# Long convolutions by FFT: complex sums of every second frequency pair left to the inverse transform's matmuls, and the first frequency's correction on ACT and GpSimd

## The chip, the cores and the metric

The kernel runs on one core of a Trainium2 chip. A core has five engines with a queue each, served in order: PE (TensorE, matmuls), DVE (VectorE), ACT (ScalarE), POOL (GpSimd) and SP (SyncE, which issues DMAs). The metric is the device time of one execution in microseconds (us).

## The reference, cut to what matters

The program is one trunk layer of a hybrid backbone: a combined input projection, a Mamba-2 scan and beside it a Hyena branch with two long convolutions, an output projection, and a retrieval over 16384 single-neuron experts. The change touches the long convolutions alone:

```
def long_conv_bidir(u, h_fwd, h_bwd, bias):
    seqlen = u.shape[1]                       # 1024 tokens, 1024 channels
    k = jnp.concatenate([h_fwd, jnp.zeros_like(h_fwd[:1]), h_bwd[:0:-1]], axis=0)
    k_f = jnp.fft.rfft(k, axis=0)
    u_f = jnp.fft.rfft(u.astype(jnp.float32), n=2 * seqlen, axis=1)
    y = jnp.fft.irfft(u_f * k_f, n=2 * seqlen, axis=1)[:, :seqlen]
    return (y + u.astype(jnp.float32) * bias.astype(jnp.float32)).astype(u.dtype)

def hyena(proj_hy, short_w, short_b, filters, filt_bias, norm_g, rows):
    u = dwconv_centred(proj_hy, short_w, short_b)
    v, x1, x2 = jnp.split(u, 3, axis=-1)
    z = x1 * long_conv_bidir(v, filters[0, 0], filters[0, 1], filt_bias[0])
    z = colmajor_to_raster(
        long_conv_bidir(raster_to_colmajor(z, rows), filters[1, 0], filters[1, 1], filt_bias[1]), rows)
    return group_rmsnorm(x2 * z, norm_g, HY_HEADS)
```

The product `u_f * k_f` is complex. Frequency 0 is a special case: its spectrum and that of the highest frequency are both real, and the kernel keeps the two in the real and the imaginary part of one entry.

## The kernel before

**Stages.** The program goes through the input projection (with the convolution filters beside it), then the scan, the convolutions and the first part of the output projection beside each other, and then the rest of the output projection and the experts. The filters' spectra lie in DRAM by the time the convolutions begin.

**A convolution job.** The channels are worked on in 8 blocks of W = 128, for each of two convolutions: 16 jobs. In a job the 1024 tokens stand as a tile of 128 partitions with 8 blocks of 128 channels. A butterfly over the 8 blocks (`butterfly`, DVE with GpSimd for two subtractions over three blocks each and ACT for two scalings) makes 8 pairs of real and imaginary input, one by one; the loop in `convs` sends each pair through three steps:

- `product`, the way forward: four fp32 matmuls of 128x128 with the matrices dft_f make the pair's spectrum hx in PSUM. The trace has two records for each such matmul.
- `spectrum`: one DVE product (L993) multiplies hx with the filter's spectrum h_k and writes h_m, which holds four blocks of 128 columns: for the real and the imaginary part (r) two terms each (j). For pair 0 of a job (n == 0) two DVE instructions on partition 0 alone (L997, L998) put frequency 0 right. Then one DVE add (L1000) sums the two terms of each part into h_p.
- `back`, the way back: four matmuls of 128x128 with dft_i add up into hy in PSUM, two for each half of hy. `take` (ACT and DVE) collects the results of 8 pairs, and `finish` (L954, L955, on GpSimd) multiplies by the gate h_g.

LAGS = (0, 1, 1) holds the second and the third step back by one pair each. h_m had NM = 2 buffers, h_p NP = 3, hx and hy NX = 2 each.

**Beside it.** `mix` runs the jobs beside three other streams: the scan (tiles s_...; its last sum on a group is L649), the search keys (ke, wq) and, once the scan is over, the first parts of the output projection (`out_some`: weights are scaled in L1091, split by ACT and GpSimd into wo_h and wo_l in `split`, L50 and L51; the matmuls are L1131 into pe, and DVE adds pe to the row in L1134, two adds for each block of 128 tokens, 32 in all). The second of these parts reads finished outputs of the convolutions (d_ohy, loaded into ot_o).

**Order.** Rates (CS, KR, TR, TL) set how many pairs the program issues beside a step of the other streams, but the order on each engine is then made by a scheduler that goes through the instructions with estimated times. It is fixed when the kernel is built; on the chip each queue is served in that order.

Of the kernel before, what the change touches and what calls it, by code (L numbers as in the profile page):

```python
# [15 lines left out]
AF = mybir.ActivationFunctionType  # L16
# [656 lines left out]
class Hyena:  # L673
# [296 lines left out]
    def convs(self):  # L970

        K, nc, wk, ps, W = self.K, self.K.nc, self.wk, self.ps, self.W
        n = D // W
        jobs = []
        for q in range(n + LQ):
            if q < n:
                jobs.append((0, q))
            if q >= LQ:
                jobs.append((1, q - LQ))
        todo = [[], [], []]  # L980

        def product(j, n, A):
            fw = self.tiles(self.PAIRS[n])[0]
            x = ps.tile([128, 2, W], F32, name="hx", bufs=NX)
            for r in range(2):
                self.mm(x[:, r], [(fw[2 * r + k], A[:, k]) for k in range(2)], "dft_f")
            return x

        def spectrum(j, n, x):

            kr = j["k"][:, 1, n]
            t = wk.tile([128, 2, 2, W], F32, name="h_m", bufs=NM)
            nc.vector.tensor_tensor(t, x[:, None].to_broadcast([128, 2, 2, W]),  # L993
                                    bass.AP(tensor=kr.tensor, offset=kr.offset,
                                            ap=[kr.ap[0], [-8 * W, 2], [8 * W, 2], [1, W]]), op=ALU.mult)
            if n == 0:
                nc.vector.tensor_scalar_mul(t[:1, 1, 1], t[:1, 0, 1], -1.0)  # L997
                nc.vector.memset(t[:1].rearrange("p r j c -> p (r j) c")[:, 1:3], 0.0)  # L998
            P = wk.tile([128, 2, W], F32, name="h_p", bufs=NP)
            nc.vector.tensor_add(P, t[:, :, 0], t[:, :, 1])  # L1000
            return P

        def back(j, n, t):
            iv = self.tiles(self.PAIRS[n])[1]
            x = ps.tile([128, 2, W], F32, name="hy", bufs=NX)
            for r in range(2):
                self.mm(x[:, r], [(iv[2 * r + k], t[:, k]) for k in range(2)], "dft_i")
            self.take(j, n, x)
            if n == 7:
                self.finish(j)  # L1010

        steps = (product, spectrum, back)
        lags = LAGS

        def advance(item):

            todo[0].append(item)
            for s in range(3):
                if len(todo[s]) > (lags[s] if item is not None else 0):
                    x = todo[s].pop(0)  # L1020
                    if x is None:
                        y = None
                    else:
                        y = steps[s](*x)
                    if s < 2:
                        todo[s + 1].append(None if x is None else (x[0], x[1], y))

        nxt = self.load(*jobs[0])
        for k in range(len(jobs)):
            j = nxt  # L1030
            if k + 1 < len(jobs):
                later = jobs[k + 1]
            for n, A in enumerate(self.butterfly(j["u"])):
                advance((j, n, A))
                if n == NL and k + 1 < len(jobs):
                    nxt = self.load(*later)
                yield
        while any(todo):
            for s in range(3):
                if todo[s]:  # L1040
                    x = todo[s].pop(0)
                    y = steps[s](*x)
                    if s < 2:
                        todo[s + 1].append((x[0], x[1], y))
            yield
# [1 line left out]

LF = 2
NA = 4
NM = 2  # L1050
NP = 3
NX = 2
NK = 2
NL = 5
# [866 lines left out]
```

## Time and profile before

| what | value |
|---|---|
| time, median of 3 runs | 4224.18 us (4220.09 to 4227.6) |
| the profiled execution's own time | 4237.9 us |
| its span, first to last instruction | 4236.2 us |
| PE busy | 3768.2 us, 89% of the span |
| DVE busy | 3415.0 us, 81% |
| POOL busy | 2054.5 us, 48% |
| ACT busy | 1389.0 us, 33% |
| mean granted clock of PE | 0.948 of full speed |

Busy shares are means over stages with different limits, so the windows further down are the better guide to the convolutions' stretch. A granted clock of 1.00 is TensorE's upper level (2.4 GHz), and a mean below that is time spent at the lower one (1.2 GHz). PE's busy time includes modelled ends of matmuls; the spacing of starts back to back is the better price of one.

### The profile page before, as it was taken

The numbers are of one execution on the slowest core, as the hardware profiler recorded it, in microseconds if no ns is written. First come the engines' busy times: TensorE is split into PE (matmuls) and PEld (weight loads), VectorE is DVE, ScalarE is ACT, GpSimd is POOL, SyncE is SP. The second block draws the span as 40 slices with busy tenths as digits, with TensorE's granted clock in tenths as the row PEclk, the third lists the DMA queues.
The fourth block names the chain that finished last, engine by engine and source line by source line (L and its number), as shares of the span: only waits on it lengthen the run. The fifth ranks groups of instructions, "written<-read, shape, count | busy, mean of one in ns | idle before, by whom it ended". The sixth has DMA issues, their size and how long they took to land.

```text
span 4236.2 us, 59519 instructions
## 1 busy us (share of the span) xinstructions
PE 3768.2 (89%) x21481; PEld 3306.9 (78%) x21481; DVE 3415.0 (81%) x6093; ACT 1389.0 (33%) x2658; POOL 2054.5 (48%) x1627
## 2 busy tenths in 40 slices
PE   5999999898887897789999877999989999989995
PEld 4787887777777786689999866888878878878884
DVE  5665887556889795589999996888878888878998
ACT  3233333325553221232236665222222222222221
POOL 2232323244434221056435444666767767767775
PEclk8999999998898998899999998999999999999998
DMA  6333433467774545567536545899989999989997
GB/s 209 103 123 103 130 112 131 136 194 208 237 232 140 165 156 166 181 226 272 209 135 220 201 169 203 316 319 325 345 294 340 326 319 335 348 305 339 344 322 258
DMA packets 509670, 974.06 MB, mean 230 GB/s; under 512 B 33771, under 2 KB 291231, under 8 KB 506432
## 3 DMA queue, kind: packets, MB, share of 16 engines
q1 hardware_dynamic: 395616, 557.25, 40.1%
q0 software_dynamic: 110880, 405.98, 26.1%
q10 hardware_dynamic: 2880, 7.03, 0.5%
q8 instruction: 169, 2.77, 0.3%
q14 instruction: 125, 1.02, 0.1%
HBM read 823.20 MB, written 146.95 MB: 229 GB/s over the span
## 4 chain that ended last, share of the span: by engine, by line
DVE 21%; PE 21%; DMA 12%; issue 7%; POOL 5%; ACT 1%; SPq 0%; POOLq 0%; DVEq 0%; ACTq 0%
PE x_acc L1671 10%; PE x_s L1631 7%; DMA x_vr<-in_peer_v_dram 6%; DVE rows L1532 3%; POOL rows L1508 2%; DMA rows<-in_peer_u_dram,ids 2%; PE pe L1131 2%; DVE r_e L1456 2%; DVE e_p L1545 1%; POOL x_vl L1603 1%; DVE r_e L1454 1%; DVE r_tmp L1343 1%; DVE r_oh L1420 1%; DVE x_ul L1592 1%; DMA rows<-in_peer_v_dram,ids 1%
## 5 line engine op out<-in xcount | busy, mean ns | idle before, releaser
L1631 PE MATMUL x_s<-fTh,x_uh 128*128 128x320 f32 x2048 | 639.6, 312 | 9.0 <-ACT x_a L1632 8.9
L1631 PE MATMUL x_s<-fTh,x_ul 128*128 128x320 f32 x2048 | 638.7, 312 | 5.9 <-DVE x_ul L1592 5.9
L1631 PE MATMUL x_s<-fTl,x_uh 128*128 128x320 f32 x2048 | 639.2, 312 | 0.0
L1671 PE MATMUL x_acc<-x_vl,x_ah 128*128 128x512 f32 x1280 | 515.9, 404 | 14.6 <-POOL x_vl L1603 14.4
L1671 PE MATMUL x_acc<-x_vh,x_ah 128*128 128x512 f32 x1280 | 448.5, 403 | 89.8 <-ACT x_vh L1602 67.0
L1545 DVE SCALAR_TENSOR_TENSOR e_p<-rows,e_a,e_p 128x1024 f32<-128x1024 f32 x381 | 489.6, 1285 | 29.3 <-DMA rows<-in_peer_v_dram,ids 22.2
L1671 PE MATMUL x_acc<-x_vh,x_al 128*128 128x512 f32 x1280 | 511.4, 401 | 0.0
L1508 POOL DMA_INDIRECT rows<-in_peer_u_dram,ids x384 | 416.1, 1084 | 173.0 <-DVE rows L1532 55.7
L1532 DVE SCALAR_TENSOR_TENSOR rows<-rows,e_p 128x1024 f32<-128x1024 f32 x384 | 455.1, 1208 | 38.5 <-DMA rows<-in_peer_u_dram,ids 38.0
L1508 POOL DMA_INDIRECT rows<-in_peer_v_dram,ids x384 | 398.9, 1039 | 146.1 <-DVE e_p L1545 64.6
L1603 POOL TENSOR_TENSOR x_vl<-x_vr,x_vh 128x512 fp32r<-128x512 f32 x256 | 339.5, 1330 | 192.7 <-ACT x_vh L1602 182.7
L1631 PEld LDWEIGHTS x_s<-fTh,x_uh 128*128 128x128 f32 x2048 | 388.3, 190 | 22.0 <-ACT x_a L1632 12.9
L1631 PEld LDWEIGHTS x_s<-fTh,x_ul 128*128 128x128 f32 x2048 | 388.5, 190 | 15.5 <-DVE x_ul L1592 6.7
L1631 PEld LDWEIGHTS x_s<-fTl,x_uh 128*128 128x128 f32 x2048 | 388.7, 190 | 9.6
L1671 PEld LDWEIGHTS x_acc<-x_vh,x_ah 128*128 128x128 f32 x1280 | 242.1, 194 | 141.9 <-ACT x_vh L1602 74.4
L1671 PEld LDWEIGHTS x_acc<-x_vl,x_ah 128*128 128x128 f32 x1280 | 248.5, 194 | 68.7 <-POOL x_vl L1603 22.7
L1602 ACT ACTIVATE x_vh<-x_vr 128x512 fp32r<-128x512 f32 x256 | 159.5, 627 | 431.6 <-DMA x_vr<-in_peer_v_dram 362.3
L1671 PEld LDWEIGHTS x_acc<-x_vh,x_al 128*128 128x128 f32 x1280 | 248.3, 194 | 49.3
L1592 POOL TENSOR_TENSOR x_ul<-x_raw,x_uh 128x1024 fp32r<-128x1024 f32 x57 | 140.9, 2472 | 275.9 <-ACT x_uh L1591 274.6
L199 PE MATMUL mm<-xh,whi 128*128 128x512 f32 (+1 forms) x784 | 265.4, 414 | 6.4 <-DVE acc L235 3.4
L199 PE MATMUL mm<-xl,whi 128*128 128x512 f32 (+1 forms) x784 | 264.6, 412 | 7.1 <-DVE xl L51 7.1
L199 PE MATMUL mm<-xh,wlo 128*128 128x512 f32 (+1 forms) x784 | 264.1, 412 | 0.4 <-POOL wlo L51 0.4
(380 smaller groups left out, 8528.3 us busy)
## 6 DMA issues: line engine op xcount, KB each, us to landing
x_raw<-in_peer_uT_dram SPq DMA_DIRECT2D x128, 512.0 KB
x_vr<-in_peer_v_dram SPq DMA_DIRECT2D x256, 256.0 KB
d_G<-r_st SPq DMA_DIRECT2D x20, 2048.0 KB
x_g<-d_G SPq DMA_DIRECT2D x32, 1280.0 KB
wraw<-in_w_mod_dram SPq DMA_DIRECT2D x32, 1024.0 KB
wraw<-in_w_in_dram SPq DMA_DIRECT2D x24, 1024.0 KB
wk_w<-d_WK SPq DMA_DIRECT2D x24, 1024.0 KB
d_kr<-h_k SPq DMA_DIRECT2D x32, 512.0 KB
```

The source lines that it names most:

```text
L199: nc.tensor.matmul(p, w[:, k], x[j][:, k, t0:t0 + n], start=(k == 0 and q == 0), stop=(k == 7 and q == 2))
L1131: nc.tensor.matmul(p, a[:, k], w[:, ss], start=(k == 0 and q == 0), stop=(k == n - 1 and q == 2))
L1343: V.match_replace(work, vals[:, 0:8], src, -3.0e38)
L1456: V.tensor_tensor(e2, io, T[:, 1, ts, None].to_broadcast([128, 8, 128]), op=ALU.is_equal)
L1508: nc.gpsimd.indirect_dma_start(out=r, out_offset=None, in_=table, in_offset=bass.IndirectOffsetOnAxis(ap=ids[:, j:j + 1], axis=0))
L1532: nc.vector.scalar_tensor_tensor(r, r, 1.0, f, op0=ALU.mult, op1=ALU.mult, accum_out=d[:, j:j + 1])
L1545: nc.vector.scalar_tensor_tensor(acc, r, a[:, j:j + 1], acc, op0=ALU.mult, op1=ALU.add)
L1592: self.pace = (nc.vector if self.turn('u', UR if self.n < NE else UP) else nc.gpsimd).tensor_sub(lo, raw, hi.bitcast(F32)).ins
L1602: nc.scalar.activation(hi, raw, AF.Copy)
L1603: self.pace = nc.gpsimd.tensor_sub(lo, raw, hi.bitcast(F32)).ins
L1631: nc.tensor.matmul(s[:, :SW], w[:, k], x[:, k, ms], start=(k == 0 and q == 0), stop=(k == 7 and q == 2))
L1671: self.K.nc.tensor.matmul(p, a[x][:, bs], v[w], start=(m == 0 and q == 0), stop=(m == SC - 1 and q == 2))
```

## The change

For the pairs with an even number (SUMS) `spectrum` returns h_m itself, and `back` gives PE the two terms of each part one after the other with the same matrix: eight matmuls into hy instead of four, and no add on DVE. The other four pairs of a job keep the add. For pair 0, which is in SUMS, the negated copy on partition 0 goes from DVE to ACT, and the memset of two blocks from DVE to GpSimd. h_m has four buffers instead of two, h_p two instead of three.

```diff
             if n == 0:
-                nc.vector.tensor_scalar_mul(t[:1, 1, 1], t[:1, 0, 1], -1.0)
-                nc.vector.memset(t[:1].rearrange("p r j c -> p (r j) c")[:, 1:3], 0.0)
+                nc.scalar.activation(t[:1, 1, 1], t[:1, 0, 1], AF.Copy, scale=-1.0)
+                nc.gpsimd.memset(t[:1].rearrange("p r j c -> p (r j) c")[:, 1:3], 0.0)
+            if n in SUMS:
+                return t
             P = wk.tile([128, 2, W], F32, name="h_p", bufs=NP)
             nc.vector.tensor_add(P, t[:, :, 0], t[:, :, 1])
             return P
...
             for r in range(2):
-                self.mm(x[:, r], [(iv[2 * r + k], t[:, k]) for k in range(2)], "dft_i")
+                self.mm(x[:, r], [(iv[2 * r + k], x) for k in range(2) for x in ([t[:, k, 0], t[:, k, 1]] if n in SUMS else [t[:, k]])], "dft_i")
...
-NM = 2
-NP = 3
+NM = 4
+SUMS = (0, 2, 4, 6)
+NP = 2
```

The first job shows the new order. On DVE, from its first product, the rows before are these (h_m is the product, h_a and h_tq are inputs of the next pairs):

```order
L993 TENSOR_TENSOR h_m<-hx,h_k 128x512
L997 TENSOR_SCALAR h_m<-h_m 1x128
L993 TENSOR_TENSOR h_m<-hx,h_k 128x512
L780 TENSOR_TENSOR h_tq<-h_te 128x384
L782 TENSOR_TENSOR h_tq<-h_te 128x384
L998 MEMSET h_m 1x256
L794 TENSOR_TENSOR h_a<-h_tx,h_ty 128x256 x2
L1000 TENSOR_TENSOR h_p<-h_m 128x256 x2
```

And now, from the same place on DVE (L1002 is the add that was L1000):

```order
L993 TENSOR_TENSOR h_m<-hx,h_k 128x512 x2
L780 TENSOR_TENSOR h_tq<-h_te 128x384
L782 TENSOR_TENSOR h_tq<-h_te 128x384
L1002 TENSOR_TENSOR h_p<-h_m 128x256
L993 TENSOR_TENSOR h_m<-hx,h_k 128x512
L794 TENSOR_TENSOR h_a<-h_tx,h_ty 128x256
L993 TENSOR_TENSOR h_m<-hx,h_k 128x512
L794 TENSOR_TENSOR h_a<-h_tx,h_ty 128x256
```

The add of pair 0 and both corrections are gone from DVE, and the third and the fourth product have moved up. On PE the first job's matmuls stood so before (hx is the way forward, hy the way back):

```order
L850 MATMUL hx<-h_tq,dft_f 128x128 x8
L596 MATMUL pe<-s_ct,s_bt 128x128
L850 MATMUL hx<-h_a,dft_f 128x128 x8
L850 MATMUL hy<-h_p,dft_i 128x128 x8
L850 MATMUL hx<-h_a,dft_f 128x128 x8
```

And now on PE, from the same place:

```order
L850 MATMUL hx<-h_tq,dft_f 128x128 x8
L596 MATMUL pe<-s_ct,s_bt 128x128
L850 MATMUL hx<-h_a,dft_f 128x128 x4
L850 MATMUL hy<-h_m,dft_i 128x128 x8
L850 MATMUL hx<-h_a,dft_f 128x128 x4
L850 MATMUL hy<-h_p,dft_i 128x128 x4
```

Pair 0 has eight matmuls on the way back, in front of the fourth pair's way forward. The correction's new place on GpSimd, in the second job, is between the scan's instructions (s_xd and s_y):

```order
L650 TENSOR_TENSOR s_y<-s_y,s_z 128x256
L772 TENSOR_TENSOR h_te<-h_u 128x384
L773 TENSOR_TENSOR h_te<-h_u 128x384
L611 TENSOR_TENSOR s_xd<-s_x,dt 128x256 x2
L650 TENSOR_TENSOR s_y<-s_y,s_z 128x256
L998 MEMSET h_m 1x256
L611 TENSOR_TENSOR s_xd<-s_x,dt 128x256 x2
```

It stands behind s_y, which waits for the scan's sum on DVE. The streams have shifted against each other as well. Of the 128 products (L993) on DVE, 60 stood in front of the scan's last sum (L649) and 42 stand there now; in front of the first add of the output projection (L1134, now L1137) it was 78 and is 67. From the twelfth such add (behind product 92) the two orders go in step again.

## Rows read from the trace of the kernel before

**Rows 1.** Windows, all engines: bounds, length, busy time of each engine (instructions), clock, DMA
```profile
core 0: us, PE busy (x) PEld busy (x) DVE busy (x) ACT busy (x) POOL busy (x), PEclk, DMA share, GB/s
1041.00:1345.00 304.00, 249.49 (x1732) 234.27 (x1731) 274.13 (x592) 151.28 (x370) 127.72 (x123) 0.88 0.66 209
1345.00:1422.00 77.00, 57.77 (x358) 50.59 (x357) 74.17 (x128) 22.36 (x42) 37.11 (x19) 0.85 0.56 178
1422.00:1505.00 83.00, 83.00 (x496) 73.13 (x496) 54.02 (x120) 13.14 (x28) 8.04 (x7) 1.00 0.46 153
1505.00:1600.00 95.00, 84.72 (x574) 76.81 (x574) 94.66 (x187) 22.05 (x42) 29.94 (x18) 0.96 0.48 149
1600.00:1668.00 68.00, 59.58 (x353) 52.61 (x352) 45.71 (x95) 9.26 (x19) 5.71 (x5) 0.95 0.49 136
```

**Rows 2.** Waits of DVE and PE, 1422 to 1668 us: total, times, longest
```profile
DVE wo L1134 <- PE pe L1131: 30.3, 14, 4.4
PE py L1121 <- DMA ot_o<-d_ohy: 7.7, 2, 6.3
```

**Rows 3.** Windows, the spectrum products of L993 on DVE: busy time (count)
```profile
1041.00:1345.00 304.00, 39.61 (x60) 0.88 0.66 209
1345.00:1422.00 77.00, 12.09 (x19) 0.85 0.56 178
1422.00:1505.00 83.00, 9.54 (x14) 1.00 0.46 153
1505.00:1600.00 95.00, 17.30 (x26) 0.96 0.48 149
1600.00:1668.00 68.00, 6.83 (x10) 0.95 0.49 136
```

**Rows 4.** Chain that ended last, 1415 to 1490 us: start, length, what
```profile
1422.10 0.89 PE hx L850 x8
1422.99 0.89 PE hy L850 x8
```

**Rows 5.** Groups of instructions, 1041 to 1668 us: busy, mean ns | idle before
```profile
L1000 DVE TENSOR_TENSOR h_p<-h_m 128x256 f32<-128x256 f32 x128 | 66.0, 528 | 1.2 <-PE hy L850 1.0
```

**Rows 6.** Single lines: duration in ns, min/median/max, first and last start
```profile
L1000 DVE TENSOR_TENSOR h_p<-h_m x128: 381/411/1494, 1083.7 to 1653.0; 128x256 f32<-128x256 f32 x128
L997 DVE TENSOR_SCALAR h_m<-h_m x16: 207/208/1042, 1081.1 to 1614.1; 1x128 f32<-1x128 f32 x16
L998 DVE MEMSET h_m<- x16: 272/272/272, 1082.9 to 1614.5; 1x256 f32 x16
```

**Rows 7.** Timeline: start, length, instruction
```profile
1239.14 2.24 POOL L955 TENSOR_TENSOR h_y<-h_y,h_g 128x512 f32<-128x512 f32 x1
1240.18 1.49 DVE L1000 TENSOR_TENSOR h_p<-h_m 128x256 f32<-128x256 f32 x1
...
1257.85 0.42 DVE L1000 TENSOR_TENSOR h_p<-h_m 128x256 f32<-128x256 f32 x1
1258.18 0.55 DVE L819 TENSOR_TENSOR h_F<-h_tg 128x384 f32<-128x384 f32 x1
```

**Rows 8.** Windows, the weight scaling of L1091 on DVE, second window
```profile
1345.00:1422.00 77.00, 12.23 (x8) 0.85 0.56 178
```

**Rows 9.** Groups on ACT and GpSimd: a 1-partition copy, a memset, the weight split
```profile
L905 ACT ACTIVATE h_k<-h_ny 1x128 f32<-1x128 f32 x16 | 4.9, 305 | 0.4
masks.py:197 POOL MEMSET ident<- 128x128 f32 x1 | 0.2, 205 | 0.3 <-POOLq L1910 0.3
L51 POOL TENSOR_TENSOR wo_l<-wo,wo_h 128x1024 fp32r<-128x1024 f32 x12 | 33.2, 2766 | 43.8 <-ACT wo_h L50 43.6
```

## The prediction

> **What bounds the kernel now.** I began with the page's busy shares and its chain of waits, which name DVE and PE alike for the whole program, and then cut the convolutions' stretch into five windows [rows 1]. The convolution work lies between 1041 us (first load into a butterfly) and 1668 us (last output); before and behind it the changed functions issue nothing. Read [rows 1] from left to right. From 1041 to 1422 us DVE is busy 274.13 of 304 and 74.17 of 77 us, PE only 249.49 and 57.77: DVE sets the pace. From 1422 to 1505 us it is the other way round: PE busy for all 83.00 us, DVE for 54.02. From 1505 to 1600 us DVE is full (94.66 of 95) with PE close behind (84.72), and in the last 68 us PE has 59.58, DVE 45.71. The waits agree: behind 1422 us DVE's longest wait is for the output projection's matmuls, 30.3 us in 14 times, and PE's for a DMA, 7.7 us [rows 2]. So DVE time removed is worth something before 1422 us, and PE time added is paid for behind it.
>
> How much convolution work lies in each window is told by the spectrum products (L993), of which each pair of frequencies has one: 60, 19, 14, 26 and 10, one of the 128 on an edge [rows 3].
>
> **The order moves too.** In the program before, 60 of the 128 products stand ahead of the scan's last sum on DVE and 78 ahead of the first add of the output projection (L1134); now it is 42 and 67. The projection's twelfth add stands behind product 92 in both, the sixteenth behind 110. So the work up to product 92 is the same, but 11 pairs pass from the DVE-bound part into the part with the projection's matmuls.
>
> **Prices.** PE: a pair's eight matmul records of the way forward, or of the way back, take 0.89 us back to back in a window with the granted clock at 1.00 (2.4 GHz, the upper of its two levels; the lower is 1.2) [rows 1, 4]; four matmuls of the program are eight records. A pair in SUMS has eight matmuls on the way back instead of four: +0.89 us, 64 times, 57 us over the stretch, or 0.445 us per pair on average. Per pair PE has had 2 x 0.89 = 1.78 us.
>
> DVE: the removed add has a mean of 528 ns [rows 5] but a median of 411 ns [rows 6], and where it runs freely the next instruction starts 0.33 us later [rows 7]. The high mean comes from cases as the one at 1240.18 us, which took 1.49 us while GpSimd ran h_y [rows 7]. I take 0.41 us, the median, since the wait behind GpSimd is one that the next DVE instruction can inherit; 0.33 and 0.53 are the ends. The Trainium skill's "SBUF — State Buffer" says the same in its section on the two separate sides: a DVE operation with two SBUF inputs and a GpSimd operation exclude each other for a whole instruction, so an add taken out of GpSimd's shadow gives its place to the next one. By that rule the add is worth about its undisturbed time; by the mean the first 46 adds would bring 46 x 0.12 = 5.5 us more. The row fits the rule, 1.49 us ending 0.29 us behind the GpSimd instruction. The correction of the first frequency takes 0.208 + 0.272 = 0.48 us of DVE [rows 6], once per job of 8 pairs. Per pair DVE saves 0.41/2 + 0.48/8 = 0.265 us.
>
> **The sum, up to product 92 (1041 to 1505 us, 464 us).** A pair without other work costs DVE 3.3 us: in the second window 74.17 less 12.23 us of weight scaling [rows 8], over 19 pairs. Ahead of the first projection add, DVE has had 348.3 us of work in 381 us. It loses 11 pairs (36 us) and 67 x 0.265 = 17.8 us: 294.5 us, and with the same 32.7 us idle 327 us. PE there has had 307.3 us, loses 11 x 1.78 = 19.6 and gains 67 x 0.445 = 29.8 us: 317.5 us in 327. That fits only barely. I let it fit because that PE time was spent at a mean granted clock of 0.88 and 0.85, below the 1.00 of the densely used window [rows 1]: a denser PE should need less. From the first add to product 92 PE gets 83.0 + 19.6 + 25 x 0.445 = 113.7 us and DVE 54.0 + 36 - 6.6 = 83.4 us: PE-bound, 114 us. Together 441 against 464 us: **-23 us**.
>
> **Behind product 92.** From 1505 to 1600 us, 26 pairs: DVE falls to 87.8, PE rises to 84.7 + 11.6 = 96.3 us against 95: +1.3 us. In the last window, 10 pairs add 4.5 us to PE, which has 8.4 us idle, nearly all of it one wait for a load that comes late [rows 1, 2]; so between 0 and 4.5, and I take 4.5, as the load hangs on work that PE has to finish first. Together **+6 us**.
>
> **The detour of the correction.** DVE -> PE becomes DVE -> ACT -> GpSimd -> PE for pair 0 of each of the 16 jobs. A 1-partition ACT copy took 305 ns, a GpSimd memset of 128x128 205 ns [rows 9]; with the 0.48 us gone from DVE that is about 0.1 us longer at least, so the term can be near nothing. At most one GpSimd instruction is just running in front, 2.77 us for wo_l [rows 9], or 3 us a job, 48 us in all. In the first window ACT is busy for half the time with instructions of 0.41 us on average (151.28/370), GpSimd for 42% with 1.04 us (127.72/123) [rows 1]: expected rest 0.5 x 0.2 + 0.42 x 0.52 = 0.3 us. I take 0.4 us a job, **+6 us**: PE's queue is in order, so what stands behind the waiting matmul (the next pair's way forward, the scan's y) waits too, and through it DVE. A second price stands on the same path: an ACT or GpSimd queue whose head itself waits holds the correction back.
>
> The other edits cost nothing: h_m with four buffers instead of two is needed because PE now reads it, and h_p with two serves half the pairs.
>
> Sum: -23 + 6 + 6 = **-11 us**. The profiled execution took 4237.9 us (1.7 us around its span of 4236.2), so it would take 4227. It lies 13.7 us over the median of the runs; taken off that median of 4224.18, the forecast is **4213 us**. Two cases of one kernel can be told apart from about 0.2%, 8.4 us.
>
> **Rivals.**
> *Full gain.* If the denser PE keeps the clock of 1.00, half of DVE's 32.7 us of idle time ahead of the projection goes as well, and the detour hides: -23 - 16 + 6 = -33, 4191 us. For it: the window at clock 1.00 has a full PE. Against: DVE's idle time up there is partly due to DMA and ACT.
> *PE becomes the bound everywhere.* PE's busy time in the stretch goes from 534.6 to 591.5 us. If whichever engine binds keeps the idle time that the binding engine had (32.7 + 0 + 0.3 + 8.4 = 41 us), the stretch takes 632 us against 627: no change, 4229 us, or 4224 with a little help from the clock. For it: 97% of PE in my own sum.
> *Slower: the detour decides.* If pair 0's matmuls stand 2.2 us a job at the head of PE's queue, 16 x 2.2 = 35: -23 + 6 + 35 = +18, 4242 us. From (23 - 6)/16 = 1.1 us a job on nothing is left of the gain. For it: GpSimd's instructions are long and wait in order; against: the order puts other matmuls between a job's first products and its way back.
> The order of the rest (behind 1668 us) changes as well; that may give or take some us in any case, and widens all of them.
>
> **How the numbers follow.** Forecast 0.45 (own range 4201 to 4222), full gain 0.14, PE-bound 0.23, slower 0.18. Faster by over 0.2% (below 4215.7): four fifths of the forecast's chance and all of the full gain, 0.50. Slower (above 4232.6): the slower rival and a third of the PE-bound case, 0.25. Within: 0.25. The range leaves out part of the full gain and of the slower rival: 4190 to 4240 us.
>
> **What would show it.** Right: in the window of the first 92 products DVE's busy share stays near 90% with 25 us less work, the clock there is over 0.9, the adds of L1134 begin some 50 us sooner, and the last window grows by a few us. Wrong: PE near 100% busy from the start with DVE waiting for hy; or many us of PE waiting for h_m's memset on GpSimd, or GpSimd's memset waiting for ACT. If the stretch ends as computed and the total does not, the order behind it is the cause.

## The result, and the profile after

| | kernel before | changed kernel |
|---|---|---|
| time, median of 7 runs each | 4233.53 us (4220.09 to 4251.90) | 4205.81 us (4197.72 to 4209.43) |
| ratio to before | 1 | 0.9935, interval 0.9922 to 0.9949 |
| profiled execution, its span | 4237.9, 4236.2 us | 4209.43, 4207.5 us |
| last output of the convolutions issued | 1667.7 us | 1654.0 us |
| from there to the end of the span | 2568.5 us | 2553.5 us |

Faster, by 0.65%. Between the medians lie 27.7 us where the forecast had 11. The last two rows part it: the convolutions' stretch became 13.7 us shorter, about what was forecast, and as much again came behind it, where the change has no instructions. (The last row compares one execution of each kernel; the barrier pair below shows how much such a part scatters.)

The five windows of the changed kernel that answer to [rows 1] (same columns, cut at the scan's last sum, the projection's first add, its twelfth, and so on; the third cut lies 3 us behind product 92 here, where in [rows 1] it lies on it):

```profile
1041.00:1282.00 241.00, 216.50 (x1542) 204.55 (x1542) 206.95 (x432) 138.31 (x345) 104.98 (x117) 0.88 0.71 226
1282.00:1378.00 96.00, 84.89 (x656) 78.88 (x657) 91.84 (x164) 30.39 (x59) 38.23 (x24) 0.98 0.61 200
1378.00:1490.00 112.00, 111.70 (x747) 101.14 (x746) 85.06 (x176) 19.38 (x42) 20.04 (x17) 1.00 0.43 139
1490.00:1586.00 96.00, 93.16 (x670) 86.62 (x669) 88.58 (x165) 22.74 (x46) 26.40 (x19) 0.98 0.48 148
1586.00:1654.00 68.00, 62.28 (x395) 55.79 (x394) 41.60 (x87) 9.41 (x19) 6.30 (x6) 0.97 0.49 135
```

And the spectrum products in them, which answer to [rows 3]:

```profile
1041.00:1282.00 241.00, 28.36 (x42) 0.88 0.71 226
1282.00:1378.00 96.00, 16.97 (x25) 0.98 0.61 200
1378.00:1490.00 112.00, 17.22 (x26) 1.00 0.43 139
1490.00:1586.00 96.00, 17.50 (x26) 0.98 0.48 148
1586.00:1654.00 68.00, 6.86 (x10) 0.97 0.49 135
```

Compare them line by line with [rows 1, 3]. The first two windows took 381 us with 79 products and now take 337 us with 67. The third, with PE full at the upper clock, took 83 us with 14 and takes 112 with 26. The last two have the same products and, from these cuts on, the same length to within 1 us; counted from product 92 they are 167 us against 163. So the gain lies ahead of product 92, where pairs changed places, and 4 us of it are given back behind.

The waits in the stretch, 1041 to 1654 us (total, times, longest), PE's first:

```profile
PE py L639 <- DVE s_y L649: 9.0, 7, 3.9
PE hx L850 <- DVE h_m L993: 8.6, 7, 2.2
PE py L1124 <- DMA ot_o<-d_ohy: 5.0, 1, 5.0
...
PE hy L850 <- DVE h_p L1002: 3.1, 5, 1.4
```

And DVE's:

```profile
DVE h_m L993 <- PE hx L850: 23.4, 17, 3.4
DVE wo L1137 <- PE pe L1134: 23.2, 12, 4.4
DVE s_e L634 <- ACT s_e L616: 19.2, 10, 6.7
```

DVE now waits for PE's way forward (hx) 23.4 us, 19.8 of them behind 1378 us, beside the full PE. Ahead of the projection's first add its longest wait and those for the convolutions' matmuls were these before (1041 to 1422 us):

```profile
DVE s_e L634 <- ACT s_e L616: 14.5, 6, 6.5
...
DVE h_m L993 <- PE hx L850: 2.7, 3, 2.4
...
DVE h_tg L803 <- PE hy L850: 2.0, 2, 1.6
...
DVE h_p L1000 <- PE hy L850: 1.0, 1, 1.0
```

and are these now (1041 to 1378 us):

```profile
DVE s_e L634 <- ACT s_e L616: 19.2, 10, 6.7
DVE h_oh L827 <- PE hy L850: 4.7, 2, 2.5
DVE h_m L993 <- PE hx L850: 3.6, 3, 1.9
```

Among PE's waits there is none for the correction. The lines of the correction and of the remaining adds (duration in ns, min/median/max), which answer to [rows 6]; under the memset, who waited for it, a single weight load:

```profile
L997 ACT ACTIVATE h_m<-h_m x16: 288/308/309, 1077.4 to 1606.5; 1x128 f32<-1x128 f32 x16
...
L998 POOL MEMSET h_m<- x16: 301/301/303, 1077.8 to 1606.9; 1x256 f32 x16
...
  PEld py L639: 1.0, 1
...
L1002 DVE TENSOR_TENSOR h_p<-h_m x64: 353/415/2119, 1081.2 to 1640.1; 128x256 f32<-128x256 f32 x64
```

The longest wait of GpSimd in the stretch is now at that memset:

```profile
POOL h_m L998 <- ACT h_m L997: 70.1, 13, 28.0
```

The prediction had named this wait as a sign of being wrong. Here it is idle time of an engine that was early at its post: PE's list shows nobody late behind it but that weight load, and DVE's list has no wait for GpSimd at all.

The whole stretch in one window, the kernel before and then the changed one:

```profile
1041.00:1667.70 626.70, 534.25 (x3505) 487.14 (x3504) 542.68 (x1118) 218.09 (x499) 208.52 (x170) 0.91 0.57 181
```

```profile
1041.00:1654.00 613.00, 568.53 (x4002) 526.98 (x4003) 514.02 (x1019) 220.22 (x511) 195.95 (x183) 0.95 0.58 184
```

PE is busy 34 us more, not the 57 that 64 pairs at 0.89 us make. Its mean granted clock rose from 0.91 to 0.95, and each matmul is shorter: a record into hy had a mean of 297 ns and has 277 (from h_m) and 281 (from h_p). DVE is busy 28.7 us less. (The barrier pair below has 26.2 us more on PE, 0.89 against 0.95, and 26.7 us less on DVE.)

### The profile page after: what moved, and what is told of

Read it like the earlier page. It is cut to its first block, busy times and chain, and to the rows that moved or that the text cites. A ratio compares the mean times of both kernels' runs of the same rounds, so it can differ in the third digit from the quotient of the medians.

```text
span 4207.5 us, 60407 instructions
## 1 busy us (share of the span) xinstructions
PE 3807.4 (90%) x21993; PEld 3346.8 (80%) x21993; DVE 3385.1 (80%) x5997; ACT 1389.8 (33%) x2674; POOL 2045.4 (49%) x1643
## 4 chain that ended last, share of the span: by engine, by line
PE 39%; DVE 22%; DMA 13%; issue 7%; POOL 6%; ACT 3%; SPq 1%; POOLq 0%; DVEq 0%; ACTq 0%
PE x_acc L1674 9%; PE x_s L1634 8%; PE mm L199 7%; DMA x_vr<-in_peer_v_dram 6%; POOL rows L1511 3%; DVE rows L1535 3%; PE pe L1134 2%; PE hy L850 2%; POOL x_vl L1606 2%; DVE r_e L1459 2%; PE tp L850 1%; DVE r_e L1457 1%; PE hx L850 1%; DMA s_e<-d_cum 1%; DMA rows<-in_peer_u_dram,ids 1%
## 5 line engine op out<-in xcount | busy, mean ns | idle before, releaser
L1674 PE MATMUL x_acc<-x_vl,x_ah 128*128 128x512 f32 x1280 | 517.2, 405 | 18.3 <-POOL x_vl L1606 18.3
L1535 DVE SCALAR_TENSOR_TENSOR rows<-rows,e_p 128x1024 f32<-128x1024 f32 x384 | 456.2, 1210 | 34.1 <-DMA rows<-in_peer_u_dram,ids 33.7
L1674 PEld LDWEIGHTS x_acc<-x_vl,x_ah 128*128 128x128 f32 x1280 | 249.8, 195 | 72.0 <-POOL x_vl L1606 26.2
L1594 ACT ACTIVATE x_uh<-x_raw 128x1024 fp32r<-128x1024 f32 x128 | 135.2, 1057 | 400.1 <-PE x_s L1634 355.4
```

The lines of the kernel that those rows point to most:

```text
L1535: nc.vector.scalar_tensor_tensor(r, r, 1.0, f, op0=ALU.mult, op1=ALU.mult, accum_out=d[:, j:j + 1])
L1594: nc.scalar.activation(hi, raw, AF.Copy)
L1674: self.K.nc.tensor.matmul(p, a[x][:, bs], v[w], start=(m == 0 and q == 0), stop=(m == SC - 1 and q == 2))
```

## The experiments

Theory A, one part of the prediction's sum: the adds taken off DVE pay, the matmuls added on PE cost less. Rival B: the order pays. The scheduler, given dearer pairs, puts fewer of them in front of the scan's end (42, not 60), the scan ends sooner, and more of the DVE-bound pairs lie beside the projection's matmuls; the work saved and added cancels. Rival C: the gain comes from the other order behind the convolutions. Eight kernels carry a barrier between the convolutions and what follows, so that nothing behind it can move up across it:

```diff
     mix(K, scan)
+    tc.strict_bb_all_engine_barrier()
     back(K)
```

All twelve at a glance. The third to fifth columns are us of the span in the profiled execution: the start of the projection's first add and of product 92, rounded up, and the issue of the last output. The null run below shows that they repeat to 3 us, to 5 if e_bar_before is counted. "Ahead" counts the products that stand ahead of the scan's last sum on DVE. The ratios are not quotients of the medians and can differ from them by 0.001.

| kernel | ahead | first add | product 92 | last output | ratio to before |
|---|---|---|---|---|---|
| before | 60 | 1423 | 1505 | 1667.7 | 1 |
| changed | 42 | 1378 | 1487 | 1654.0 | 0.9935 (0.9922 to 0.9949) |
| e_bar_before | 60 | 1423 | 1505 | 1669.5 | 1.0016 (1.0004 to 1.0029) |
| e_bar_after | 42 | 1379 | 1487 | 1654.2 | 0.9978 (0.9967 to 0.9988) |
| e_bar_dve | 87 | 1492 | 1417 | 1636.0 | 1.0017 (1.0005 to 1.0028) |
| e_bar_pe | 46 | 1390 | 1494 | 1657.3 | 1.0001 (0.9990 to 1.0012) |
| e_bar_order | 42 | 1374 | 1491 | 1653.4 | 0.9953 (0.9937 to 0.9968) |
| e_bar_dve_order | 42 | 1385 | 1484 | 1643.8 | 0.9964 (0.9947 to 0.9981) |
| e_bar_sums | 42 | 1380 | 1490 | 1659.3 | 0.9955 (0.9939 to 0.9972) |
| e_bar_detour | 43 | 1390 | 1489 | 1658.7 | 1.0025 (1.0009 to 1.0042) |
| e_null | 60 | 1421 | 1503 | 1664.6 | 1.0005 (0.9991 to 1.0019) |
| e_order | 42 | 1373 | 1490 | 1651.6 | 1.0001 (0.9986 to 1.0017) |
| e_order_d | 30 | 1364 | 1491 | 1656.7 | 0.9993 (0.9981 to 1.0006) |
| e_early9 | 42 | 1377 | 1481 | 1641.3 | 0.9907 (0.9886 to 0.9928) |

**e_bar_before and e_bar_after: both kernels with the barrier.** Only in this pair is the order behind the barrier the same, instruction by instruction.

> The kernel before with an all-engine barrier between the convolutions' stage and the output projection. With it the order of everything behind the barrier is the same, instruction by instruction, as in its twin e_bar_after, so the pair differs in the stage alone. Both theories: the barrier stops the loads that run ahead into the next stage, so 5 to 20 us slower than before (ratio 1.001 to 1.005). Its first part, up to the last output of the convolutions, stays at about 1668 us of its span.

> The changed kernel with the same barrier. Theory A (the changed kernel's gain is some 14 us in the convolutions' stretch, the rest is the luck of another order behind it): 14 us faster than e_bar_before (ratios 0.0033 apart), and equal lengths behind the barrier. Rival B (the stage itself is worth all of the gain, since what follows it inherits an earlier start of its loads or a better state): 24 to 28 us faster than e_bar_before.

Medians 4243.66 and 4225.35 us: 18.3 us, of which 15.3 are in the stretch (1669.5 against 1654.2). Without the barrier it is 27.7 and 13.7. So with one order behind, the median follows the stretch to 3 us, nearer to theory A of e_bar_after (14 us) than to its rival (24 to 28). The 10 us by which this pair's gain is smaller than the 27.7 then belong to the order behind; that is an estimate from sets whose runs spread over 12 to 32 us. The two profiles do not show it: behind the last output they took 2583.6 and 2562.6 us in one and the same order, 21 us apart. So one profile's part behind the stretch is no measure of an order, and the 2568.5 and 2553.5 us above are none either.

**e_bar_dve: the adds gone, and nothing put on PE.** The second term of the SUMS pairs is left out.

> As e_bar_after, but the pairs in SUMS use the first of the two terms alone: four matmuls, no add. It leaves out half of those pairs' sums, so it has DVE's relief without the 256 extra matmuls. By my sum (the extra matmuls are paid for behind product 67, where PE binds: 11 + 1 + 4.5 us, and hidden before): 15 to 20 us faster than e_bar_after. Rival (PE has room everywhere once the clock is up): within 5 us of e_bar_after. Rival (PE binds from the start): 35 us or more faster than e_bar_after.

```diff
-... for x in ([t[:, k, 0], t[:, k, 1]] if n in SUMS else [t[:, k]])]
+... for x in ([t[:, k, 0]] if n in SUMS else [t[:, k]])]
```

Less work than in either kernel of the comparison, and 1.0017: not the 15 to 20 us faster than e_bar_after that were expected, but 14.3 slower by the medians. All three expectations missed. The pairs are cheap now, and the scheduler puts 87 of them ahead of the scan's end. Its windows to the projection's first add, its twelfth, and the last output:

```profile
1041.00:1491.00 450.00, 367.31 (x2629) 342.86 (x2627) 413.79 (x849) 203.13 (x477) 177.78 (x172) 0.90 0.64 195
1491.00:1563.00 72.00, 71.58 (x389) 61.37 (x390) 40.35 (x83) 9.39 (x19) 7.97 (x7) 1.00 0.49 160
1563.00:1636.00 73.00, 66.00 (x373) 56.93 (x371) 48.52 (x82) 14.56 (x25) 17.29 (x9) 0.95 0.41 123
```

In the second window DVE is busy 40 of 72 us beside a full PE: there are few pairs left to put there. The projection's last add comes at 1685 us, against 1670 before and 1656 in the changed kernel. (The last output, 1636, comes ahead of it and is no end of the stretch here.) Theory A alone cannot be right.

**e_bar_pe: the opposite.** Every pair keeps its add on DVE, and PE has the additional matmuls all the same.

> As e_bar_after, but the add into h_p is made for all pairs, though the pairs in SUMS do not read it: the extra matmuls without DVE's relief from adds. By my sum DVE gets 64 x 0.41 = 26 us back, of which some 14 in front of the output projection's first add are on the path: 14 to 20 us slower than e_bar_after. If PE bound everywhere: within 5 us of e_bar_after.

```diff
-            if n in SUMS:
-                return t
...
-            return P
+            return t if n in SUMS else P
```

More work than before on PE and none less in adds, and still its last output comes 12.2 us sooner than that of e_bar_before, since only 46 products stand ahead of the scan's end. For B. (Against e_bar_after it is 3.1 us later and 9.0 us slower by the medians, less than the 14 to 20 expected and more than the rival's 5.)

**e_bar_order and e_bar_dve_order: the order alone.** The products are held behind the scan's sums as they stand in the changed kernel: in e_bar_order with the work of the kernel before, unchanged; in e_bar_dve_order with that of e_bar_dve, which leaves out the second term.

> The work of the kernel before, with the barrier, in the changed kernel's order of streams: each spectrum product is queued on DVE behind the scan's sum that stands in front of it in the changed kernel (issue order only, no wait), so 42 products instead of 60 stand ahead of the scan's end, and 60 instead of 78 ahead of the first projection add. Theory C (the stage's gain is made by the order, which the scheduler changed because it took the pairs for dearer): as e_bar_after, ratio 0.996 to 0.999, last output of the convolutions at 1650 to 1658 us. Rival D (it is made by DVE's 34 us less work): as e_bar_before, ratio 1.000 to 1.003, last output at 1665 to 1672 us.

> e_bar_dve (half of the summed pairs' terms left out: DVE's relief without the extra matmuls) in the changed kernel's order of streams, by the same queueing. By theory C, e_bar_dve was slow only by its order (87 products ahead of the scan's end), and here the price of the 256 extra matmuls shows cleanly: 10 to 18 us faster than e_bar_after (ratio 0.9935 to 0.9955). If the extra matmuls cost nothing: ratio 0.997 to 0.999. If the order is not what made e_bar_dve slow: 1.001 or more again.

```diff
+BEHIND = (12, 12, 12, 12, 12, 13, 13, 14, 15, 16, ..., 30, 30, 31, 32)
...
-        nc.vector.tensor_add(y[:, gs], y[:, gs], py[:, :256])
+        K.sums.append(nc.vector.tensor_add(y[:, gs], y[:, gs], py[:, :256]).ins)
...
+            s = BEHIND[min(len(K.prods), len(BEHIND) - 1)]
+            with K.tc.issue_after(K.sums[min(s, len(K.sums)) - 1]):
+                p = nc.vector.tensor_tensor(t, ...)
+            K.prods.append(p.ins)
```

e_bar_order has the last output at 1653.4 us, e_bar_after at 1654.2: the order gives all of the stretch's gain with no work changed. The total, 0.9953, even lies below e_bar_after's 0.9978 (another order behind the barrier). And with the order held, the second terms that e_bar_dve_order lacks are worth 10.4 us of stretch (1643.8 against e_bar_after's 1654.2): the price of the additional matmuls. Its other side is e_bar_dve_order against e_bar_order, the adds and the correction off DVE and nothing put on PE: 9.6 us (1653.4 to 1643.8). The two cancel. (At the projection's last add, which is the later end in e_bar_dve_order, they are 6.9 and 4.4 us. The total of e_bar_dve_order, 0.9964, lies between its two theories. The order is held at the scan's end alone: ahead of the first add stand 60 products in e_bar_order, 67 in e_bar_after and 68 in e_bar_dve_order.)

**e_bar_sums and e_bar_detour: the correction.** The first has the sums on PE and the correction on DVE as before. The second puts eight more ACT copies into each job's correction.

> The changed kernel with the barrier, and the first frequency's correction left on DVE as before: the sums' part of the change alone. Forecast of the prediction (the detour costs 6 us, DVE saves 16 x 0.48 = 7.7 us, some 5 on the path): within 4 us of e_bar_after. If ACT and GpSimd did it for nothing: 5 to 8 us slower than e_bar_after (ratio 0.999 to 1.000).

> The changed kernel with the barrier, and the negated copy on ACT followed by eight more of them (the sign turns each time, so the value stays): the detour of each job is 8 x 0.2 to 0.3 = 2 us longer, and nothing else. If pair 0's matmuls stand at the head of PE's queue until the correction lands (the slower rival's mechanism): 16 x 2 = 25 to 35 us slower than e_bar_after. If other matmuls stand between: within 8 us of e_bar_after.

```diff
                 nc.scalar.activation(t[:1, 1, 1], t[:1, 0, 1], AF.Copy, scale=-1.0)
+                for _ in range(8):
+                    nc.scalar.activation(t[:1, 1, 1], t[:1, 1, 1], AF.Copy, scale=-1.0)
```

With the correction on DVE the last output comes 5.1 us later than in e_bar_after, so the detour is at least no loss there. Eight more copies a job are 8 x 0.308 = 2.5 us, 39 us over 16 jobs. In the trace the detours grew by more, since other ACT instructions came to stand between the copies: from a job's first copy to the end of its last copy or memset they take 101 us in all, against 13.4 in e_bar_after. (GpSimd's memset follows the first copy alone; what PE has to wait for in addition is the last copy.) The last output comes 4.5 us later. In the trace of e_bar_detour the row on the copies shows how little of PE waited for them (PEld is PE's weight load):

```profile
L999 ACT ACTIVATE h_m<-h_m x128: 288/308/312, 1077.2 to 1614.6; 1x128 f32<-1x128 f32 x128
...
  POOL s_y L619: 6.5, 1
  PEld hy L850: 1.4, 2
...
  PE hy L850: 0.5, 2
```

So all but 4.5 of the 88 us are hidden, where the unchanged detour has 0.84 us a job. (The 5.1 and the 4.5 us are little above what profiles of one kernel differ by.) The totals of these two, 0.9955 and 1.0025, say otherwise than their stretches, which differ by 0.6 us; from the last output to the end of the span it is 2546.6 us in the one profile and 2580.4 in the other. The work there is the same, the order another.

**e_null, e_order, e_order_d, e_early9: without a barrier.** These four share one set of runs of the kernel before.

> The kernel before, unchanged, once more: a ruler for what lies behind the convolutions. If the part behind the last output of the convolutions repeats from execution to execution (theory A), it takes 2568 us again to within 3 us, and the last output stands at 1668 us. If it scatters (theory B), the last output stands at 1668 us to within 2 us and the part behind it differs by 5 to 15 us from the 2568.5 us of the profile of before. Ratio 1.000 by both, within 0.002.

The last output comes 3.1 us sooner than in the first profile of this kernel (expected at 1668), the part behind it takes 2571.2 us instead of 2568.5. Its theory A fits, but is not settled: both profiles fell on executions of nearly one time (4237.9 and 4237.5 us), and those of before go from 4220.53 to 4244.36 in this set. What can be compared behind the stretch are medians.

> The instructions of the kernel before, none of them changed, with the spectrum products held behind the scan's sums as they stand in the changed kernel (42 products ahead of the scan's last sum, not 60), without a barrier behind the convolutions. Theory 'the order pays': the last output comes at 1653 us as in the changed kernel (1654), and the total is 0.993 of before, 4206 us on the scale of the first comparison, or a few us less, since PE has 57 us of matmuls less and DVE 25 us of adds more. Rival 'the sums pay, the order only with them': with the adds left on DVE, the gain is at most half of it: ratio 0.997.

The stretch is as expected, 1651.6 us, and the total is not: 1.0001, both theories missed. The median, 4229.56 us, is 4.2 under before where the stretch gained 16.1, so by the medians 12 us were given back behind it (9 if the stretch is compared with e_null's 1664.6). (Its profiled execution took 4213.17 us, the shortest of 12 that go up to 4250.48; the loss does not stand in this profile.) The windows to the first add, the twelfth, and the last output, and the products in them:

```profile
1041.00:1372.00 331.00, 266.61 (x1783) 243.52 (x1783) 294.67 (x602) 161.10 (x384) 135.97 (x129) 0.87 0.67 214
1372.00:1490.00 118.00, 118.00 (x796) 107.67 (x795) 102.58 (x231) 24.13 (x50) 20.93 (x16) 0.99 0.48 152
1490.00:1651.60 161.60, 144.06 (x921) 127.21 (x919) 134.23 (x284) 30.96 (x61) 37.07 (x23) 0.97 0.50 147
```

```profile
1041.00:1372.00 331.00, 39.91 (x60) 0.87 0.67 214
1372.00:1490.00 118.00, 21.82 (x32) 0.99 0.48 152
1490.00:1651.60 161.60, 24.32 (x36) 0.97 0.50 147
```

Beside the changed kernel's windows this parts order and work. Up to the first add the changed kernel does 7 products more (67 against 60) in 6 us more; at the 3.3 us of a DVE-bound pair that is worth 23 - 6 = 17 us, an estimate. Then PE is full in both and most of it goes: 25 pairs in 109 us (1378 to 1487) against 32 in 118 (1372 to 1490). At product 92, with equal work done, the changed kernel is 3 us ahead, and from there to the last output it takes 167 us instead of 162. In all the work itself is worth 2.4 us less than nothing, within what profiles repeat to.

> As the run before, but with the products held further behind the scan: 30 of 128 stand ahead of its last sum instead of 42, so that the scan ends sooner and more pairs lie beside the projection's matmuls. If the gain grows with the lag (the scan and the projection are simply the longer path), the last output comes another 5 to 10 us sooner than with 42: 1645 us, ratio 0.991. If PE is then full beside the projection and DVE is left with nothing, it comes later: 1660 us, ratio 0.996. I expect the second, since in the changed kernel PE has no idle time between 1378 and 1490 us.

The scan's end and the first add come sooner still (1364), product 92 at the same time (1491), the last output 5.1 us later than in e_order. As expected of a PE that is already full beside the projection: 42 products ahead are better than 60, and 30 are no better than 42. (The last output was expected at 1660 us and the ratio at 0.996; the total, 0.9993, follows the stretch as little as e_order's.)

> The changed kernel with the sums on PE and the correction on ACT and GpSimd in the first 9 of the 16 jobs alone; the last 7 jobs keep the adds and the correction on DVE. These jobs lie beside the projection, where PE is full and DVE is not. If PE's time counts there (my sum had 0.445 us a pair from the first projection add on, about 56 pairs, 25 us on PE, some 13 us less of it with the order in step from product 92), the last output comes 5 to 12 us sooner than the changed kernel's 1654 us, ratio 0.990 to before. Rival 'the clock gives it back': a less dense PE falls to the lower clock there and the gain is under 3 us, ratio 0.9935.

```diff
-            if n in SUMS:
+            if n in SUMS and j["i"] < EARLY:
                 return t
...
-NM = 4
+NM = 3
+EARLY = 9
-NP = 2
+NP = 3
```

(`back` has the same condition; later jobs have the correction on DVE as before. The numbers of buffers changed with it, and no run has the two apart.) The windows to the first add, the twelfth's neighbourhood at 1490, and the last output:

```profile
1041.00:1377.00 336.00, 294.73 (x2200) 275.97 (x2200) 300.06 (x595) 168.02 (x404) 140.84 (x141) 0.94 0.69 219
1377.00:1490.00 113.00, 111.72 (x731) 100.39 (x730) 95.66 (x204) 20.87 (x43) 19.66 (x14) 1.00 0.47 153
1490.00:1641.30 151.30, 134.90 (x855) 118.99 (x854) 126.40 (x264) 29.44 (x57) 35.32 (x21) 0.97 0.47 138
```

The first window is the changed kernel's (337 us, 2198 matmul records). Behind it 28 pairs have their add on DVE again; PE has 25 us of matmuls less, and the last output comes 12.7 us sooner, just past the 12 expected at most (the projection's last add 9.6 us sooner). Against e_order, which has no added matmuls at all, it is 10.3 us: in the early jobs, where DVE binds, the exchange of adds for matmuls pays. The clock does not give it back: 0.97 against 0.98 and 0.97 in the windows behind 1490 us. The total is 4191.29 us (4185.16 to 4200.80), 0.9907 of before. It beats before clearly; the changed kernel did not run beside it, and its 0.9935 comes from another set, so between the two the 12.7 us of stretch are the better evidence.

## Why the prediction was right, and where it was not

**The sum.** Its three terms, against the trace (the events as in the table):

| term | forecast | measured |
|---|---|---|
| 1041 us to the projection's first add | 381 to 327 us, -54 | 381 to 337 us, -44 |
| first add to product 92 | 114 us | 109 us |
| both: up to product 92 | -23 | -18 |
| behind product 92 | +6 | +4.3 |
| the correction's detour | +6 | no place of its own: hidden |
| stretch | -11 | -13.7 |

The direction, the place and the size of the stretch's gain were right: DVE-bound pairs moved into the projection's part, which then was PE-bound at the upper clock. Two terms were mis-sized and cancelled. In the step on the part up to the first add, "with the same 32.7 us idle" failed: DVE was busy 298.8 us (206.95 + 91.84), 4 more than computed, and idle 38 of 337, 5.5 more than taken. By the waits shown above the additional idle time is for ACT (s_e, 19.2 us instead of 14.5) and for PE's way back (hy, 4.7 instead of 3.0); the waits for hx hardly grew there (3.6 instead of 2.7). "That fits only barely" was the warning, but by DVE's direct waits PE, busy 301 of the 337 us, accounts for some 3 of the 10 us. 5 us came back between the first add and product 92. The detour's 6 us did not come, though its length was sized well: 13.5 us in 16 jobs from the copy's start to the memset's end, 5.8 more than 16 x 0.48. What failed is that it stands on the path: other matmuls stand between pair 0's product and its way back, which the prediction had as an argument against its slower rival and left out of its own term. Of its signs, the clock up to product 92 was 0.93 (over 0.9 named), the projection's adds began 44 us sooner (some 50 named), DVE was busy 85% with 21 us less work (near 90% and 25 named), and the last window did not grow.

**What pays.** The prediction took relief of DVE and shift of order in one sum and did not ask what each gives alone. Its own method applied to e_order gives 348.3 - 18 x 3.3 + 32.7 = 322 us to the first add, then 83 + 18 x 1.78 = 115 us: product 92 at 1478, 27 us sooner, which is more than with the work changed. The trace says 1490. The 18 pairs are known from e_order alone, but the prediction's own 11 say the same: without the change of work 348.3 - 36 + 32.7 = 345 us to the first add and 83 + 19.6 = 102.6 behind it, 17 us sooner, which leaves -7 + 6 + 6 = +5 us to the work. So its own terms already held that the order is the gain, and that moving adds to PE gives nothing in the sum over the stretch; that reading was missed. Measured, the order alone is worth 16 us of stretch (e_bar_order against e_bar_before, e_order against before; 13 against e_null), and in that order the work taken off DVE is worth 9.6 us and the matmuls added on PE cost 10.4. e_early9 takes the first without much of the second.

**DVE's prices.** By the median, 0.265 us a pair, 128 pairs save 34 us; DVE's busy time fell by 28.7. The 64 adds that went had 31.1 us (66.0 less 64 x 0.545), the correction 7.7, 38.8 in all: some 10 us of it came back in other instructions. That agrees with the choice of the median over the mean, and with the Trainium skill's "SBUF — State Buffer" in its section on the two separate sides: a DVE instruction with two SBUF inputs and a GpSimd instruction that reads SBUF exclude each other, and whichever starts first holds the ports for its whole length. An add out of that shadow can then leave its place to the next such instruction. The add of 2119 ns is such a case, it ends 0.28 us behind a GpSimd instruction that reads SBUF:

```profile
1113.07 2.82 POOL L503 TENSOR_TENSOR s_fw<-s_fw,etot 128x1024 f32<-128x1024 f32 x1 [0.54 <-DVE s_fw L514]
1114.05 2.12 DVE L1002 TENSOR_TENSOR h_p<-h_m 128x256 f32<-128x256 f32 x1
```

And the instructions that grew, at the same count, are the butterfly's, also with two SBUF inputs; each before and after:

```profile
L794 DVE TENSOR_TENSOR h_a<-h_tx,h_ty 128x256 f32<-128x256 f32 x64 | 29.3, 462 | 0.7 <-PE hx L850 0.7
L794 DVE TENSOR_TENSOR h_a<-h_tx,h_ty 128x256 f32<-128x256 f32 x64 | 35.4, 554 | 0.0
L766 DVE SCALAR_TENSOR_TENSOR h_tx<-h_te,h_u 128x256 f32<-128x256 f32 x32 | 13.2, 413 | 0.0
L766 DVE SCALAR_TENSOR_TENSOR h_tx<-h_te,h_u 128x256 f32<-128x256 f32 x32 | 17.7, 553 | 0.0
```

Others shrank (h_F from a mean of 609 to 549 ns), and no run held GpSimd off them, so that they inherited just this wait is not shown.

**The rivals.** *Full gain*: the clock did reach 0.98 and 1.00 behind the scan's last sum, but stayed at 0.88 in the first window, and DVE's idle time ahead of the projection grew; no. *PE-bound everywhere*: it computed 632 us for the stretch from 591.5 us of PE work; the trace has 613 and 568.5. The idle time of PE (44.5 us) was close to the 41 taken; what failed was the work, since PE's busy time grew by 34 and not by 57 us. *Slower, the detour decides*: refuted, no wait of PE's for it but 1.0 us of a weight load, and a longer one costs 4.5 us of stretch.

**The total.** The forecast of 4213 lies 7.2 us above the median, within its range, but by luck in part. The seven runs of before have a median 9.4 us above that of the three it started from, and 14 of the 27.7 us of gain come from behind the stretch. The prediction named that possibility and its reading: the stretch ends as computed and the total does not, so the order behind is the cause. The runs bear it out as far as this: with the order behind held equal, medians follow the stretch to 3 us (the barrier pair, one pair); where it differs, median totals stray from the stretch's gain by -16 us (e_early9: 42.5 against 26.4) to +12 (e_order: 4.2 against 16.1) without a barrier, with 6 to 9 us of uncertainty either way on such a total, and e_bar_sums and e_bar_detour lie 33.7 us apart on stretches that differ by 0.6. That the other 14 us are made by the order behind is so far argued from these, not shown for the changed kernel itself. What in the orders behind makes one better than another stays open: no experiment held the stretch and changed only that.

## What to carry to other kernels

Where a scheduler sets the order from estimated times, a change of one instruction's cost is first of all a change of order; hold the order fixed and change the work, then the other way round, before either is believed. Price each instruction by the window in which it will stand: over the whole stretch the work taken off DVE gained 9.6 us and the matmuls put on PE cost 10.4, while the same exchange in the first nine jobs alone gained 10 us, so apply it only where it gains. A kernel with a long, unrelated part behind the change needs a milestone inside the span, since the total can move by as much for reasons of order there.

## What the runs showed of the hardware

- A fuller PE ran at a higher granted clock, 0.95 against 0.91 over the stretch (0.89 in e_null and e_bar_before), and 57 us of matmuls added 34 us of busy time. Up to the first add the kernels in the new order without these matmuls had 0.87 (e_order, e_bar_dve_order) and 0.86 (e_bar_order), the changed kernel and e_bar_after 0.91. In the changed kernel the difference lies behind the scan's last sum: 0.98 with PE busy 84.89 of 96 us, where e_order had 0.86 with 56.70 of 78; ahead of it both had 0.88. One window with the same products can differ by 0.04 between two kernels' profiles all the same (0.88 in the changed kernel, 0.92 in e_early9, up to the scan's last sum).
- A GpSimd memset of 1x256 took 301 ns, longer than the 205 ns of a 128x128 one [rows 9]; on DVE it had taken 272 [rows 6]. So a row of 256 on one partition cost GpSimd more than 128 columns on all 128 partitions.
